# Query and key norms of the attention by one GpSimd power, and the first score product ahead of the last query transposes

## The chip, the cores and the metric

One core of a Trainium2 chip runs the whole program. The metric is the device time of one execution in microseconds (us), given as the median of the runs. A second figure, the span, is the time in the profiled execution from its first to its last recorded instruction.

## The reference, cut to what matters

The program is a two-layer diffusion transformer on 512 image tokens (the latents) and 256 context tokens, 1024 wide, all in fp32. Layer 0 mixes the tokens by attention with 16 query heads of 64 columns in 4 groups, one key and value head for each group; layer 1 mixes them by a recurrent scan. Every layer ends in a gated feed-forward block. The change lies in layer 0, between the projection of queries and keys and the first scores:

```
def rms_norm(x, w):
    xf = x.astype(jnp.float32)
    y = xf * lax.rsqrt(jnp.mean(xf * xf, axis=-1, keepdims=True) + NORM_EPS)
    return (y * w.astype(jnp.float32)).astype(x.dtype)
...
    def queries(h):
        t = h.shape[1]
        q = (h @ w_q).reshape(b, t, ATTN_KV_HEADS, ATTN_GROUP, HEAD_DIM).transpose(0, 2, 3, 1, 4)
        return rms_norm(q, q_norm)
...
    q_l = apply_axial_rope(queries(h_lat), rope)
    k_l, v_l = keys_values(h_lat)
    k_l = apply_axial_rope(k_l, rope)
    k_c, v_c = keys_values(h_ctx)
    k_all = jnp.concatenate([k_c, k_l], axis=2)
```

Each query and key head of each token is divided by the root of its mean square over 64 columns, weighted, and turned by a position angle (only the latents are turned). Then come scores, softmax, and the weighted sum of the values.

## The kernel before, in words

Tokens are handled as six tiles of 128, two to a unit: `tp` 0 and 1 are the latents, `tp` 2 is the context. A matrix product in fp32 is three products of a high and a low part (`mm3`, lines 112 to 114), so each operand is split first: ACT casts the high part (`whi_...`, L88), DVE or POOL subtracts for the low part (`wlo_...`, L91). For the query weights each group `g` has two halves of 128x1024, `wq{g}0` and `wq{g}1`; DVE makes their low parts.

The stage in question goes through 15 norm units. Twelve are query units `q{g}{tp}` (`q_first`), and between those of group 0 stand the three key units k0, k1, k2 (`k_first`). For each query unit TensorE (PE) runs 48 products `q<-...` into a PSUM bank. Then `qk_norm_rope` does, for 128 tokens x 2 tiles x 4 heads x 64 columns:

- ACT squares the bank (L510), DVE sums over 64 columns into `ss`, 128x8 (L513), and scales (L514).
- ACT takes the root (L515). DVE takes the reciprocal (L516) and makes one refining step (L517 to L520).
- DVE multiplies it in (`qhat`, L522). Then the turn: DVE multiplies by the cosine (`qrot`, L532), POOL by the sine (`qsin`, four pieces, L537), DVE adds (L541). The context has one multiplication by the weight on POOL instead (L526).
- For a query, DVE casts the high part (`qd`, L585) and POOL subtracts the low part (L586). For a key this is `kd` (L556) and `kl` (L557).

The second half of a unit is done later. PE transposes (`ptq` L592 for queries, `ptk` L567 for keys), and ACT moves the result from PSUM into `qT` or `kT` (L595, L571, L576); DVE moves one part of the keys (`kT<-ptk`, L577). The list `later` holds these second halves back by `Q_LAG` units. What is left at the end of the projections is issued in the loop of L654: query units q22, q30, q31 and q32. A score product `sc` (four products, L645 and L646) takes a query tile and all keys. PE also has filler work: `pa` (L181, the modulation vectors) and `rx` (L671, the residual's transposes).

The code states which instructions there are and what each needs. The framework's scheduler decides statically the order on each engine, so an edit can move instructions that it doesn't name. At run time each engine works strictly in its order.

Of the kernel before, what the change touches and what calls it, by code (L numbers as in the profile page):

```python
# [8 lines left out]
F32 = mybir.dt.float32  # L9
F32R = mybir.dt.float32r  # L10
U8 = mybir.dt.uint8
AF = mybir.ActivationFunctionType
ALU = mybir.AluOpType
# [3 lines left out]
P = 128  # L17
# [30 lines left out]
def kernel(  # L48
# [10 lines left out]
    PE, DVE, ACT, POOL = nc.tensor, nc.vector, nc.scalar, nc.gpsimd  # L59
    dma = nc.sync.dma_start  # L60

    def pool(name, es=None, **kw):
        return (es or ctx).enter_context(tc.tile_pool(name=name, bufs=1, reuse_waits="tile", **kw))
# [5 lines left out]
    def psum_pool(**bufs):  # L69
        es = ExitStack()  # L70
        psums["pool"], psums["bufs"] = pool(f"psum{len(bufs)}", es, space=PSUM), bufs
        return es


    def s2(name):
        if "s2" in psums:
            return psums["s2"].tile([P, 1024], F32, tag="s2", bufs=3, name=name)
        return psums["pool"].tile([P, 1024], F32, tag="s2", bufs=psums["bufs"]["s2"], name=name)
# [76 lines left out]
    mhalf = cst.tile([P, 1], F32, name="mhalf")  # L155
# [173 lines left out]
    qst = pool("qkvst", qes, side="right")  # L329
# [172 lines left out]
    def qk_norm_rope(src, tp, nm, eng=POOL):  # L502
        w, cw, sw = tabs[nm]

        def tmp(tag, bufs=1):
            tt = qst.tile([P, 512], F32, tag=tag, bufs=bufs, name=tag)
            return tt.rearrange("p (t h d) -> p t h d", t=2, d=HD)

        sq = tmp("qrot", 2)
        ACT.activation(sq, src, AF.Square)  # L510
        sst = qst.tile([P, 3, 8], F32, tag="ss", bufs=2, name="ss")
        ss, sr, sa = sst[:, 0], sst[:, 1], sst[:, 2]
        DVE.tensor_reduce(ss, sq.rearrange("p t h d -> p (t h) d"), op=ALU.add, axis=AX.X)  # L513
        DVE.tensor_scalar(ss, ss, 1.0 / HD, EPS, op0=ALU.mult, op1=ALU.add)  # L514
        ACT.activation(sr, ss, AF.Sqrt)  # L515
        DVE.reciprocal(sr, sr)  # L516
        DVE.tensor_tensor(sa, sr, sr, op=ALU.mult)  # L517
        DVE.tensor_tensor(sa, sa, ss, op=ALU.mult)
        DVE.tensor_scalar(sa, sa, -0.5, 1.5, op0=ALU.mult, op1=ALU.add)
        DVE.tensor_tensor(ss, sr, sa, op=ALU.mult)  # L520
        qh = tmp("qhat")
        DVE.tensor_tensor(qh, src, ss.rearrange("p (t h) -> p t h", t=2).unsqueeze(3).to_broadcast([P, 2, 4, HD]),  # L522
                          op=ALU.mult)
        r = tmp("qrot", 2)
        if tp == 2:
            eng.tensor_tensor(r.rearrange("p t h d -> p (t h) d"), qh.rearrange("p t h d -> p (t h) d"),  # L526
                               w.unsqueeze(1).to_broadcast([P, 8, HD]), op=ALU.mult)
            return r
        sn = tmp("qsin")
        for tt in range(2):  # L530
            t = tp * 2 + tt
            DVE.tensor_tensor(r[:, tt], qh[:, tt], cw[:, t].unsqueeze(1).to_broadcast([P, 4, HD]), op=ALU.mult)  # L532
            sn5 = sn[:, tt].rearrange("p h (a b i) -> p h a b i", a=2, b=2)
            q5 = qh[:, tt].rearrange("p h (a b i) -> p h a b i", a=2, b=2)
            t5 = sw[:, t].rearrange("p (a b i) -> p a b i", a=2, b=2)
            for b in range(2):
                POOL.tensor_tensor(  # L537
                    sn5[:, :, :, b], q5[:, :, :, 1 - b],
                    t5[:, :, b].unsqueeze(1).to_broadcast([P, 4, 2, 16]), op=ALU.mult,
                )  # L540
        DVE.tensor_tensor(r, r, sn, op=ALU.add)  # L541
        return r
# [8 lines left out]
    def k_first(tp):  # L551
        r = qk_norm_rope(kraw[tp].rearrange("p t (h d) -> p t h d", d=HD), tp, "k")
        kd = qst.tile([P, 2, KVH, 2, HD], F32R, tag="sp", bufs=3, name="kd")
        kl = qst.tile([P, 2, KVH, HD], F32R, tag="spl", name="kl")
        for i in range(2):
            DVE.tensor_copy(kd[:, :, :, i].rearrange("p t h d -> p (t h) d"), r.rearrange("p t h d -> p (t h) d"))  # L556
        POOL.tensor_tensor(kl, r, kd[:, :, :, 0].bitcast(F32), op=ALU.subtract)  # L557

        def second():
            kds = [kd[:, :, g].rearrange("p t a d -> p t (a d)") for g in range(KVH)]  # L560
            kds += [kl[:, :, 2 * i : 2 * i + 2].rearrange("p t a d -> p t (a d)") for i in range(KVH // 2)]
            cs = slice(tp * 256, tp * 256 + 256)
            for i in range(0, len(kds), 2):
                pt = bank("ptk")
                for j in range(2):
                    for tt in range(2):
                        PE.transpose(pt[:, (2 * j + tt) * P : (2 * j + tt + 1) * P],  # L567
                                     kds[i + j][:, tt].bitcast(F32), ident)
                pg = pt.rearrange("p (g t) -> p g t", g=2)
                if i < KVH:  # L570
                    ACT.copy(kTt[:, i : i + 2, cs], pg)  # L571
                    continue
                for j in range(2):
                    dst = kTt[:, KVH + j : 2 * KVH : 2, cs]
                    rows = slice(j * HD, (j + 1) * HD)
                    ACT.copy(dst[0:HD], pg[rows])  # L576
                    DVE.tensor_copy(dst[HD:P], pg[rows])  # L577

        return second

    def q_first(g, tp, ps):
        eng = DVE if g == KVH - 1 and tp == 2 else POOL
        r = qk_norm_rope(ps.rearrange("p (t h d) -> p t h d", t=2, d=HD), tp, "q", eng)
        qd = qst.tile([P, 2, 4, 2, HD], F32R, tag="sp", bufs=3, name="qd")
        DVE.tensor_copy(qd[:, :, :, g % 2], r)  # L585
        eng.tensor_tensor(qd[:, :, :, 1 - g % 2], r, qd[:, :, :, g % 2].bitcast(F32), op=ALU.subtract)  # L586

        def second():
            for tt in range(2):
                pt = bank("ptq")  # L590
                for j in range(4):
                    PE.transpose(pt[:, j * P : (j + 1) * P],  # L592
                                 qd[:, tt, j].rearrange("p a d -> p (a d)").bitcast(F32), ident)
                t = tp * 2 + tt
                ACT.copy(qT[g][:, :, t * P : (t + 1) * P], pt.rearrange("p (h t) -> p h t", h=4))  # L595

        return second
# [36 lines left out]
    def key_tiles(t):  # L634
        return range(4, 6) if t >= NLT else range(NT)

    def score_mm(h, t):
        g, j = h // 4, h % 4
        keys = key_tiles(t)
        nk, k0 = len(keys) * P, keys[0] * P  # L640
        q = qT[g][:, j, t * P : (t + 1) * P]
        ps = s2("sc")
        for a in range(0, nk, 512):
            e = min(nk, a + 512)
            PE.matmul(ps[:, a:e], q, kTh[g][:, k0 + a : k0 + e], start=True, stop=False)  # L645
            PE.matmul(ps[:, a:e], q, kTl[g][:, k0 + a : k0 + e], start=False, stop=True)  # L646
        return ps
# [1 line left out]
    dfill.drain()  # L649
    pes.close()  # L650
    pes = psum_pool(s2=2, b=2, t=2)
    early = {}
    for i, f in enumerate(later):
        f()  # L654
        if i == 0:
            early[0, i] = score_mm(0, i)
    qes.close()

    hpool = pool("hT", side="right")
# [1007 lines left out]
    sa, sb = scan_head(GH - 2), scan_head(GH - 1)  # L1667
# [72 lines left out]
```

## Time and profile before

| | before |
|---|---|
| device time, median of 3 runs | 1858.29 us (1854.88 to 1858.45) |
| the profiled execution | 1857.14 us |
| its span | 1855.4 us |
| busy PE | 1787.0 us, 96% |
| busy DVE | 1219.8 us, 66% |
| busy ACT | 766.8 us, 41% |
| busy POOL | 542.2 us, 29% |

The profiled execution has 1.74 us outside its span. A busy engine is one with an instruction under way. PE is busy nearly all the time over the whole program, but not in every stage: the norm units fill the time from about 75 to 182 us, and there it has gaps.

### The profile page before, as it was taken

What the parts mean: (1) busy time and instruction counts of PE and PEld (TensorE: products, weight loads), DVE (VectorE), ACT (ScalarE), POOL (GpSimd) and SP (SyncE); (2) the same over time, 40 slices, a digit from 0 to 9 for tenths busy, and PEclk for the clock granted to TensorE, in tenths of its full rate; (3) what the DMA queues carried; (4) which work ended last, traced back from release to release, by engine and by line L of the source; (5) the groups of instructions that cost most, each with busy time, mean ns of one, the idle gap of its engine ahead of it and who ended that gap; (6) DMA issues with size and microseconds to landing.
All of it is one profiled execution on the core that took longest, in us unless ns stands there. A gap on an engine that the chain in (4) does not pass through costs nothing.

```text
span 1855.4 us, 30297 instructions
## 1 busy us (share of the span) xinstructions
PE 1787.0 (96%) x11929; PEld 1630.3 (88%) x11929; DVE 1219.8 (66%) x2097; ACT 766.8 (41%) x1465; POOL 542.2 (29%) x508
## 2 busy tenths in 40 slices
PE   8989999998899999999999989999998999999998
PEld 6778688987899989998988989898897799898997
DVE  3576688888778777878756465655738774344443
ACT  3333777776633424242445333233333432222234
POOL 1244254444512414141314253344535100000000
PEclk9989999999999999999999999999999999999999
DMA  9433410002134242435231212213211253333321
GB/s 319 167 115 88 161 58 24 23 2 68 30 91 120 73 121 75 142 98 165 68 114 45 69 47 80 68 47 91 80 46 35 86 159 98 91 87 95 97 88 55
DMA packets 213198, 166.41 MB, mean 90 GB/s; under 512 B 7696, under 2 KB 190144, under 8 KB 213056
## 3 DMA queue, kind: packets, MB, share of 16 engines
q1 hardware_dynamic: 212768, 163.43, 28.6%
q8 instruction: 94, 1.54, 0.3%
q10 hardware_dynamic: 288, 1.05, 0.1%
q14 instruction: 48, 0.39, 0.1%
HBM read 162.36 MB, written 2.10 MB: 89 GB/s over the span
## 4 chain that ended last, share of the span: by engine, by line
PE 80%; DVE 9%; POOL 4%; ACT 4%; issue 2%; DMA 1%; POOLq 0%; SPq 0%; DVEq 0%; ACTq 0%
PE ffo L112 5%; PE ffo L113 5%; PE ffo L114 5%; PE ffi L112 4%; PE ffi L113 4%; PE ffi L114 4%; PE pt L703 3%; PE x L112 2%; PE x L113 2%; PE x L114 2%; PE lv L1541 2%; PE hz L112 2%; PE hz L113 2%; PE hz L114 2%; PE y L114 1%
## 5 line engine op out<-in xcount | busy, mean ns | idle before, releaser
L112 PE MATMUL ffi<-fnh,whi_fi 128*128 128x256 f32 x704 | 198.9, 283 | 0.1
L113 PE MATMUL ffi<-fnl,whi_fi 128*128 128x256 f32 x704 | 198.0, 281 | 1.0 <-DVE fnl L1221 1.0
L114 PE MATMUL ffi<-fnh,wlo_fi 128*128 128x256 f32 x704 | 197.8, 281 | 0.0
L113 PEld LDWEIGHTS ffi<-fnl,whi_fi 128*128 128x128 f32 x704 | 133.2, 189 | 1.5 <-DVE fnl L1221 1.4
L112 PEld LDWEIGHTS ffi<-fnh,whi_fi 128*128 128x128 f32 x704 | 132.7, 189 | 0.5 <-issue 0.3
L114 PEld LDWEIGHTS ffi<-fnh,wlo_fi 128*128 128x128 f32 x704 | 132.8, 189 | 0.0
L676 DVE SCALAR_TENSOR_TENSOR hT<-ffo,modc,hT 128x512 f32<-128x512 f32 (+1 forms) x106 | 66.9, 635 | 90.9 <-PE ffo L114 90.9
L1548 POOL TENSOR_TENSOR KD<-KD,tot 128x384 f32<-128x384 f32 x96 | 101.3, 1078 | 68.2 <-ACT kc L1531 66.6
L278 POOL TENSOR_TENSOR rc<-rc,mhalf 128x2 f32<-128x2 f32 (+2 forms) x7 | 6.2, 886 | 377.6 <-DVE rc L276 377.6
L693 POOL TENSOR_SCALAR pf<-pf,st 128x768 f32<-128x768 f32 (+1 forms) x96 | 73.3, 766 | 128.1 <-DVE st L692 91.7
L88 ACT CAST whi_fi<-raw_fi 128x1024 fp32r<-128x1024 f32 x44 | 46.2, 1051 | 146.4 <-PE ffi L113 68.7
L114 PE MATMUL ffo<-gh,wlo_w 128*128 128x512 f32 (+1 forms) x304 | 102.6, 338 | 0.0
L113 PE MATMUL ffo<-gl,whi_w 128*128 128x512 f32 (+1 forms) x304 | 102.4, 337 | 0.0
L112 PE MATMUL ffo<-gh,whi_w 128*128 128x512 f32 (+1 forms) x304 | 101.7, 337 | 0.0
L91 DVE TENSOR_TENSOR ptl<-pt,pth 128x384 fp32r<-128x384 f32 (+1 forms) x160 | 79.8, 523 | 12.4 <-ACT pth L88 11.2
L1531 ACT COPY kc<-KD 128x256 f32<-128x256 f32 x112 | 43.0, 414 | 102.8 <-PE lv L1541 37.1
L689 DVE TENSOR_REDUCE st<-sc 128x1 f32<-128x768 f32 (+1 forms) x96 | 74.1, 772 | 15.2 <-PE sc L646 12.5
L88 ACT CAST pth<-pt 128x384 fp32r<-128x384 f32 (+1 forms) x160 | 69.8, 460 | 34.4 <-PE pt L703 22.6
L235 DVE SCALAR_TENSOR_TENSOR adacc<-adw,csil,adacc 128x512 f32<-128x512 f32 x98 | 81.6, 846 | 2.6 <-DMA adw<-in_ada_w_dram 1.9
L1548 DVE TENSOR_TENSOR QD<-QD,tot 128x256 f32<-128x256 f32 x96 | 55.5, 618 | 41.2 <-PE lv L1541 40.5
L691 ACT ACTIVATE pf<-sc,st 128x768 f32<-128x768 f32 (+1 forms) x96 | 73.3, 764 | 19.3 <-DVE st L689 18.3
L703 PE MATMUL pt<-ident,pf 128*128 128x128 f32 x448 | 72.1, 275 | 5.2 <-DVE ptl L91 3.9
(833 smaller groups left out, 5985.1 us busy)
## 6 DMA issues: line engine op xcount, KB each, us to landing
raw_fi<-in_ffn_w_in_dram SPq DMA_DIRECT2D x44, 512.0 KB, 3.7
adw<-in_ada_w_dram SPq DMA_DIRECT2D x40, 512.0 KB, 4.4
adw<-in_ada_w_dram SPq DMA_DIRECT2D x80, 256.0 KB, 3.1
raw_hz<-in_hgrn_w_in_dram SPq DMA_DIRECT2D x14, 512.0 KB, 3.7
raw_fo<-in_ffn_w_out_dram SPq DMA_DIRECT2D x16, 448.0 KB, 3.8
adr<-in_ada_w_dram SPq DMA_DIRECT2D x16, 256.0 KB, 4.7
adr<-in_ada_w_dram SPq DMA_DIRECT2D x8, 512.0 KB, 6.8
raw_wq<-in_attn_w_qkv_dram SPq DMA_DIRECT2D x8, 512.0 KB, 4.9
```

The costliest lines, as they stand in the source:

```text
L88: ACT.copy(hi, src)
L91: (eng or DVE).tensor_tensor(lo, src, hi.bitcast(F32), op=ALU.subtract)
L112: PE.matmul(ps, ahi, bhi, start=first, stop=False, **kw)
L113: PE.matmul(ps, ahi, blo, start=False, stop=False, **kw)
L114: PE.matmul(ps, alo, bhi, start=False, stop=last, **kw)
L235: pin(DVE.scalar_tensor_tensor(a, raw, cc, a, op0=ALU.mult, op1=ALU.add))
L676: DVE.scalar_tensor_tensor(hT[o][:, a:e], ps, mcol(layer, ch, o, v), hT[o][:, a:e], op0=ALU.mult, op1=ALU.add)
L689: DVE.tensor_reduce(st3[:, 0:1], ps[:, :nk], op=ALU.max, axis=AX.X, negate=True)
L691: ACT.activation(pf, ps[:, :nk], AF.Exp, bias=st3[:, 0:1], accum_out=st3[:, 1:2])
L693: POOL.tensor_scalar(pf, pf, st3[:, 2:3], 1.0, op0=ALU.mult, op1=ALU.mult)
L703: PE.transpose(pt[:, i * P : (i + 1) * P], pf[:, (i0 + i) * P : (i0 + i + 1) * P], ident)
L1548: eng.tensor_tensor(view, view, f, op=ALU.mult)
```

## The change

The root, the reciprocal and the refining step (six instructions, one on ACT and five on DVE) become one POOL instruction, `ss` to the power -0.5 (`mhalf` is a constant of -0.5). The tile `ss` has 128x8 elements instead of three such rows. At the end of the projections the score product (0,0) is written ahead of the four second halves that are left over, and (0,1) stands where (0,0) stood.

```
-        sst = qst.tile([P, 3, 8], F32, tag="ss", bufs=2, name="ss")
-        ss, sr, sa = sst[:, 0], sst[:, 1], sst[:, 2]
+        ss = qst.tile([P, 8], F32, tag="ss", bufs=2, name="ss")
         DVE.tensor_reduce(ss, sq.rearrange("p t h d -> p (t h) d"), op=ALU.add, axis=AX.X)
         DVE.tensor_scalar(ss, ss, 1.0 / HD, EPS, op0=ALU.mult, op1=ALU.add)
-        ACT.activation(sr, ss, AF.Sqrt)
-        DVE.reciprocal(sr, sr)
-        DVE.tensor_tensor(sa, sr, sr, op=ALU.mult)
-        DVE.tensor_tensor(sa, sa, ss, op=ALU.mult)
-        DVE.tensor_scalar(sa, sa, -0.5, 1.5, op0=ALU.mult, op1=ALU.add)
-        DVE.tensor_tensor(ss, sr, sa, op=ALU.mult)
+        POOL.tensor_tensor(ss, ss, mhalf.to_broadcast([P, 8]), op=ALU.pow)
...
-    early = {}
+    early = {(0, 0): score_mm(0, 0)}
     for i, f in enumerate(later):
         f()
         if i == 0:
-            early[0, i] = score_mm(0, i)
+            early[0, 1] = score_mm(0, 1)
```

Lines from L516 on are six lower in the new file. Over the program DVE has 75 instructions less (15 units by five), POOL has 15 more. ACT loses the 15 roots and three loads of a function table: two ahead of the first two roots, and the one ahead of the first exponential (L691). Behind the first few score products the order is the same as before on every engine.

The first place is one unit on POOL, in the steady part: the sine product and subtraction of q31 and what follows. Before:

```order
L537 TENSOR_TENSOR qsin<-qhat,swq 128x8x16 x4
L586 TENSOR_TENSOR qd<-qrot,qd 128x8x64
L537 TENSOR_TENSOR qsin<-qhat,swq 128x8x16 x4
L586 TENSOR_TENSOR qd<-qrot,qd 128x8x64
L693 TENSOR_SCALAR pf<-pf,st_2018 128x768
```

The same place of the changed kernel:

```order
L531 TENSOR_TENSOR qsin<-qhat,swq 128x8x16 x4
L580 TENSOR_TENSOR qd<-qrot,qd 128x8x64
L514 TENSOR_TENSOR ss<-ss,mhalf 128x8
L531 TENSOR_TENSOR qsin<-qhat,swq 128x8x16 x4
L580 TENSOR_TENSOR qd<-qrot,qd 128x8x64
L514 TENSOR_TENSOR ss<-ss,mhalf 128x8
L687 TENSOR_SCALAR pf<-pf,st_1948 128x768
```

The power of each unit stands behind the subtraction of the unit ahead of it.

The second place is DVE among the first units, from the `qhat` of key unit k1 to that of query unit q01. Before:

```order
L522 TENSOR_TENSOR qhat<-kraw,ss 128x512
L532 TENSOR_TENSOR qrot<-qhat,cwk 128x256 x2
L577 CAST kT<-ptk 64x2x256
L541 TENSOR_TENSOR qrot<-qrot,qsin 128x512
L513 TENSOR_REDUCE ss<-qrot 128x8
L556 CAST kd<-qrot 128x8x64 x2
L577 CAST kT<-ptk 64x2x256
L514 TENSOR_SCALAR ss<-ss 128x8
L91 TENSOR_TENSOR wlo_wq_1140<-raw_wq_1138,whi_wq_1139 128x1024
...
L522 TENSOR_TENSOR qhat<-q_872,ss 128x512
```

The changed kernel from the same `qhat` of k1 on, to that of k2:

```order
L516 TENSOR_TENSOR qhat<-kraw,ss 128x512
L526 TENSOR_TENSOR qrot<-qhat,cwk 128x256 x2
L535 TENSOR_TENSOR qrot<-qrot,qsin 128x512
L550 CAST kd<-qrot 128x8x64 x2
L512 TENSOR_REDUCE ss<-qrot 128x8
L513 TENSOR_SCALAR ss<-ss 128x8
L516 TENSOR_TENSOR qhat<-q_862,ss 128x512
L571 CAST kT<-ptk 64x2x256
...
L512 TENSOR_REDUCE ss<-qrot 128x8
L571 CAST kT<-ptk 64x2x256
L535 TENSOR_TENSOR qrot<-qrot,qsin 128x512
```

The two moves of k0's keys out of PSUM (`kT`) stood ahead of q01's norm and now stand behind its `qhat`; the first two low parts of `wq1` stood inside q01's norm and now stand behind the `qhat` of k2, further down.

The third place is PE at the end of the query projections, from the transposes of q22 on (`ptq`, eight for each unit). Before:

```order
L592 MATMUL ptq<-ident,qd 128x128 x16
L645 MATMUL sc<-kT,qT_705 128x512
L646 MATMUL sc<-kT,qT_705 128x512
L645 MATMUL sc<-kT,qT_705 128x256
L646 MATMUL sc<-kT,qT_705 128x256
L592 MATMUL ptq<-ident,qd 128x128 x8
L671 MATMUL rx_2040<-ident,hT_2004 128x128 x2
L592 MATMUL ptq<-ident,qd 128x128 x8
L671 MATMUL rx_2040<-ident,hT_2004 128x128 x4
```

The changed kernel:

```order
L586 MATMUL ptq<-ident,qd 128x128 x8
L639 MATMUL sc<-kT,qT_705 128x512
L640 MATMUL sc<-kT,qT_705 128x512
...
L586 MATMUL ptq<-ident,qd 128x128 x8
L639 MATMUL sc<-kT,qT_705 128x512
L640 MATMUL sc<-kT,qT_705 128x512
...
L586 MATMUL ptq<-ident,qd 128x128 x16
L181 MATMUL pa<-adw_2045,cpad 32x256 x4
```

Score product (0,0) now stands ahead of q30's transposes, and (0,1) where (0,0) was. Their PSUM banks have changed with them: (0,0) had the banks of q31 and q32, and has now an idle one and that of q22; (0,1) has those of q31 and q32.

## Rows read from the trace of the kernel before

**Rows 1.** Windows: us, then busy us (x instructions) of PE, PEld, DVE, ACT, POOL; PEclk

```profile
93.00:139.00 46.00, 36.94 (x298) 33.58 (x297) 36.68 (x84) 17.35 (x33) 20.31 (x24) 0.90 0.36 116
139.00:186.00 47.00, 43.53 (x354) 42.19 (x354) 30.95 (x72) 16.20 (x33) 19.71 (x24) 0.95 0.32 89
```

**Rows 2.** Waits of PE from 60 to 240 us: total, times, longest

```profile
PE q L113 <- DVE wlo_wq L91: 5.1, 1, 5.1
PE sc L645 <- DVE qhat L522: 3.5, 1, 3.5
PE pta L189 <- ACT kT L571: 1.7, 1, 1.7
```

**Rows 3.** Chain that ended last, 70 to 240 us: start, us, what

```profile
172.78 2.15 POOL qsin L537 x4
174.95 0.70 DVE qrot L541
176.80 0.75 DVE ss L514
```

**Rows 4.** Tile ss by line: ns min/median/max, first and last start

```profile
L515 ACT ACTIVATE ss<-ss x15: 208/209/211, 77.4 to 177.6; 128x8 f32<-128x8 f32 x15
L517 DVE TENSOR_TENSOR ss<-ss x15: 166/167/1249, 77.9 to 178.1; 128x8 f32<-128x8 f32 x15
```

**Rows 5.** Timeline of DVE: start, us, what [idle before it]

```profile
93.63 0.69 DVE L522 TENSOR_TENSOR qhat<-kraw,ss 128x512 f32<-128x512 f32 x1
...
102.78 0.69 DVE L522 TENSOR_TENSOR qhat<-q,ss 128x512 f32<-128x512 f32 x1
...
134.10 1.22 DVE L91 TENSOR_TENSOR wlo_wq<-raw_wq,whi_wq 128x1024 fp32r<-128x1024 f32 x1
...
142.50 0.69 DVE L513 TENSOR_REDUCE ss<-qrot 128x8 f32<-128x512 f32 x1 [1.27 <-ACT qrot L510]
...
169.77 0.78 DVE L514 TENSOR_SCALAR ss<-ss 128x8 f32<-128x8 f32 x1
...
171.94 0.69 DVE L522 TENSOR_TENSOR qhat<-q,ss 128x512 f32<-128x512 f32 x1
...
178.93 0.69 DVE L522 TENSOR_TENSOR qhat<-q,ss 128x512 f32<-128x512 f32 x1
```

**Rows 6.** Timeline of POOL, the same columns

```profile
98.34 1.31 POOL L557 TENSOR_TENSOR kl<-qrot,kd 128x512 fp32r<-128x512 f32 x1 [1.80 <-PE ptq L592]
...
169.22 1.30 POOL L586 TENSOR_TENSOR qd<-qrot,qd 128x512 fp32r<-128x512 f32 x1 [1.33 <-DVE qd L585]
```

**Rows 7.** Powers on POOL elsewhere: the groups of L375, L278 and L1600

```profile
L375 POOL TENSOR_TENSOR rs<-rs,mhalf x6: 548/550/570, 7.2 to 14.5; 128x1 f32<-128x1 f32 x6
L278 POOL TENSOR_TENSOR rc<-rc,mhalf x7: 696/865/1189, 441.7 to 1848.9; 128x2 f32<-128x2 f32 x3, 128x3 f32<-128x3 f32 x2, 128x4 f32<-128x4 f32 x2
L1600 POOL TENSOR_TENSOR oss<-oss,mhalf x8: 1007/1314/1325, 1073.6 to 1448.9; 128x4 f32<-128x4 f32 x8
```

**Rows 8.** Timeline of PE, the same columns

```profile
99.41 0.63 PE L567 MATMUL ptk<-ident,kd 128*128 128x128 f32 x4 [0.74 <-DVE kT L577]
101.52 0.66 PE L567 MATMUL ptk<-ident,kd 128*128 128x128 f32 x4 [1.49 <-ACT qT L595]
...
135.38 0.58 PE L113 MATMUL q<-wlo_wq,hnh 128*128 128x256 f32 x1 [5.14 <-DVE wlo_wq L91]
...
179.67 0.50 PE L645 MATMUL sc<-kT,qT 128*128 128x512 f32 x1 [3.46 <-DVE qhat L522]
```

**Rows 9.** Windows of 5 us, the columns of the first group

```profile
100.00:105.00 5.00, 3.51 (x26) 1.75 (x26) 4.09 (x10) 3.88 (x7) 1.04 (x3) 0.73 0.51 133
135.00:140.00 5.00, 4.62 (x22) 4.62 (x23) 4.07 (x10) 0.21 (x1) 1.98 (x2) 0.51 0.57 162
```

**Rows 10.** Timeline of ACT, the same columns

```profile
76.09 1.28 ACT L515 ACT_TABLE_LOAD   x1
...
185.56 1.28 ACT L691 ACT_TABLE_LOAD   x1
```

## The prediction

> **What bounds the kernel now.** Over the whole program PE is busy 96%, so I looked for the stage where it is not. The windows show it: from 93 to 139 us PE is busy for 36.94 of 46 us at a granted clock of 0.90, and from 139 to 186 us for 43.53 of 47 at 0.95 [rows 1]. These are the norm units. The list of waits says what PE lacks there: 5.1 us once for the low part of a query weight (`wlo_wq`), 3.5 us once for the last `qhat`, 1.7 us for a move of keys [rows 2]; two shorter ones, 0.74 and 1.49 us, stand ahead of the transposes of k1 [rows 8]. The chain of waits runs through POOL and DVE: sine product, addition, norm [rows 3]. So DVE's norm units, one after another, set this stage: PE waits in the middle because DVE comes late to a weight (134.10 us, rows 5), and at the end because the last `qhat` is late.
>
> **The cost of one norm.** The scale of one unit ends at 169.77 + 0.78 = 170.55 and `qhat` starts at 171.94 [rows 5]: 1.39 us for root, reciprocal, refinement and two changes of engine. In their place comes a hand-over to POOL (0.15 us, from the end of `qhat` at 172.63 to the sine product at 172.78), the power, and a hand-over back (0.03 us, from 174.92 to 174.95) [rows 3, 5]. A power on 128x8 does not occur in the trace. The rows give 550 ns for one column, 696 for two, 1007 at best for four: (1007 - 550) / 3 = 152 ns for each column [rows 7]. So eight take about 1007 + 4 x 152 = 1615 ns. That makes 0.15 + 1.62 + 0.03 = 1.80 us against 1.39: **each unit's chain is 0.4 us longer**, although DVE has 0.9 us less work in it. DVE's saved time buys nothing, because in the steady units DVE has nothing between scale and `qhat` in the new order: it waits.
>
> Bounds of the power: below, eight columns cost no more than four, 1.01 us, which is 0.2 us less than now for a unit; above, powers run into others' work as those at 1325 ns did against 1007 [rows 7], so 1.62 x 1.32 = 2.13 us, 0.9 us more than now. I take 1.62, since the steps from one to four columns are even and nothing else is named in the order beside the power in a steady unit.
>
> The Trainium skill, GPSIMD Engine Reference, section 3 (and its opening), calls this engine the wrong choice for ordinary elementwise arithmetic, with Vector about twice as fast. By that, a power would take twice the 0.17 us of a DVE step, 0.34 us, a unit would gain 0.9 us, and the sum would come to about 1844 (a rival below). The trace disagrees: a single column already takes 0.55 us [rows 7].
>
> In the steady units the power isn't delayed by POOL's queue: it stands behind the subtraction of the unit before, which ended at 169.22 + 1.30 = 170.52, and DVE's scale already ended only then, at 170.55 [rows 5, 6].
>
> **The early units.** Here the change also removes a table load of 1.28 us ahead of the first root [rows 10], so k0 gains 1.28 - 0.4 = 0.9 us; q00 gives 0.4 back. In k1's norm one step lasted 1249 ns instead of 167 beside a subtraction on POOL [rows 4]; the new order puts k1's power ahead of that subtraction, so k1 gains 1.1 - 0.4. Its `qhat` moves from 93.63 [rows 5] to about 92.4. Then, with the durations of the rows: sine product 0.84 after `qhat`, 2.15 long; addition 0.7; the cast of `kd` I put at 0.7, like the addition; scale held by the subtraction `kl`, 1.31 [rows 3, 5, 6]; power and hand-overs 1.80. That is 92.4 + 0.84 + 2.15 + 0.7 + 0.7 + 1.31 + 1.8 = 99.9 for q01's `qhat`, against 102.78: 2.9 us earlier.
>
> But the moves of k0's keys, which PE's transposes of k1 need, stood ahead of q01's norm and now stand behind its `qhat`: `qhat` and one move, then cosine products of about 1.0, a sum of 0.7, the second move 0.7. They end at 99.9 + 0.7 + 0.7 + 1.0 + 0.7 + 0.7 = 103.7. PE was ready at 99.41 - 0.74 = 98.67 [rows 8]: **it waits 5.0 us in place of 0.74**. The next four transposes wait for q00's `qT` on ACT, which stands behind a squaring that needs the buffer of q01's subtraction; on POOL this now stands behind the power of k2. Addition 104.4, scale and cast to 105.0, power to 106.6, subtraction to 107.9, squaring and move 0.6 each: 109.1. PE would be there at 104.3, so it waits 4.8 us in place of 1.49. Together PE starts q10 about (5.0 - 0.74) + (4.8 - 1.49) = 7.6 us later.
>
> What it gets back: the 1.7 us wait for keys goes (k2's moves come ahead of what delayed them), and DVE reaches the weight of q20 about as now or earlier: 2.9 us ahead at q01, 0.4 back in each of four units, 134.10 - 1.3, and 1.22 long, at about 134. PE wants it at 135.38 - 5.14 + 7.6 - 1.7 = 136.1, so **the 5.1 us wait vanishes**. The clock: after the 5.14 us wait, PE had five us at a granted clock of 0.51 [rows 9], the lower of its two levels (1.2 of 2.4 GHz), which cost 2.4 us; from 100 to 105 us it had 0.73, which cost 1.35. The two new waits have only four transposes between them, so I count one slow stretch, 2.4 - 1.35 = 1.05 us. Before, PE was in effect at 135.38 + 2.4 = 137.8; after, at 136.1 + 1.05 = 137.2. **q20 starts 0.6 us earlier.** DVE waited for that unit's bank (idle 1.27 ahead of 142.50, rows 5), so the 0.6 is passed on.
>
> **The late units.** From 142.50 to the last `qhat` at 178.93 [rows 5] DVE's chain runs through six units (q20 to q32): 6 x 0.4 = **+2.4 us**.
>
> **The score product.** The four products of (0,0) took 0.8 us from 179.67, after 3.46 us of idle PE [rows 8]. Now their banks are free early and they run in that gap; it starts a little later and is as long. That is worth up to 0.8 us. (0,1) takes the old place, and brings forward work that came later. Behind it, `rx` now waits for the first exponential to free the bank; that one no longer has its table load of 1.28 us [rows 10]. I keep half, **-0.4**.
>
> **Sum.** -0.6 + 2.4 - 0.4 = +1.4 us on the profiled 1857.14, so 1858.5 us. That execution is 1.15 us under the median of 1858.29; 0.2%, or 3.7 us, is about what a measurement of this kernel can tell from no change, so the forecast is no measurable change.
>
> **Rivals.**
>
> *Slower by a dear power.* At 2.13 us a unit is 0.9 longer: 6 x 0.9 = 5.4 late; five early units delay PE by a further 5 x 0.5 = 2.5. With -0.6 - 0.4 this makes +6.9, so 1864. For it: the median of the eight powers at L1600 is 1314 ns, so most of them are not at the best [rows 7]. Against: the new order leaves DVE idle beside the power. It decides from about 1.85 us on (11 units x 0.23 = 2.5 on top of 1.4). A sentence of the Trainium skill bears on it: the GPSIMD Engine Reference, section 1, says that the engine's memory interface is shared with Vector, with contention for Vector's instructions with two inputs; the 1249 ns step agrees.
>
> *Slower by the clock.* The two early waits cost two slow stretches, 2.4 us more; or the weight of q20 is late all the same. 1861 to 1863.
>
> *Faster by a cheap power.* At 1.01 us a unit is 0.2 shorter: 6 x -0.2 = -1.2 late, 5 x -0.6 = -3 early, -0.6 and -0.8: -5.6, so 1851.5. Against: four even steps say otherwise.
>
> *Faster by ordinary arithmetic on POOL.* If a power cost as much as two of DVE's steps of 167 ns [rows 4], 0.34 us, a unit would be 0.87 us shorter, 1.28 less than in my sum; 11 units and the +1.4 make -12.7, so 1844.5. Against: 0.55 us for one column. This is the rule of the GPSIMD page of the Trainium skill named above.
>
> *Faster in the early part.* The power is as I say, but the two long waits are not: the moves of keys run earlier, and PE gains the 5.1 us wait and its slow stretch. If half of the 7.6 us goes, q20 is bound by its weight, at 134 to 135, some 3 us earlier than before: 1857.14 - 3 + 2.4 - 0.8 = 1855.7 at least, and 1853 with the slow stretch gone.
>
> *It does nothing.* The saved work was never what DVE waited for and the longer chain is met by slack: 1857.
>
> **Numbers.** The forecast and the last rival together 0.45, the dear power 0.20, the clock 0.10, the cheap power 0.09, ordinary arithmetic 0.01, the early part 0.15. Some of the last ends within 0.2%, some of the dear power too. So faster 0.24, same 0.46, slower 0.30. The range reaches from the cheap power to the dear one, 1851.5 to 1865.
>
> **What would show it.** The group of the power: median near 1.62 us. Scale to `qhat`: 1.8 us. PE's waits: two of about 5 us ahead of the transposes of k1, none for `wlo_wq`, and one of 3 to 4 us ahead of score product (0,1). The clock under 0.8 between 100 and 115 us and near 1.00 from 135 to 140. The last `qhat` 1.8 us later, near 180.7. I would be wrong first of all through the power's duration, since it counts 11 times; next, if the early waits of PE are not followed by the loss of the 5.1 us one.

## The result and the profile after

The changed kernel takes 1861.34 us (median of 10 runs, 1858.33 to 1862.84), the kernel before 1856.53 us in the same comparison (10 runs, 1854.56 to 1858.54). The ratio is 1.0026, 95% interval [1.0018, 1.0034]: 4.8 us slower, with the whole interval above 1. The forecast of 1858.5 us was "no measurable change"; the time is inside its range, 2.8 us above its point, and beyond the 0.2% in which I had placed it. The miss is larger than these 2.8 us: the forecast was a change of +1.4 us, and the change cost 4.8.

The profiled execution has a span of 1861.1 us. Windows of the changed kernel in the columns of [rows 1]:

```profile
93.00:139.00 46.00, 35.35 (x286) 32.20 (x285) 31.25 (x49) 18.06 (x30) 29.57 (x31) 0.85 0.31 101
139.00:186.00 47.00, 40.93 (x329) 40.21 (x328) 25.45 (x42) 11.51 (x21) 31.77 (x31) 0.94 0.24 73
```

PE is busy for 1.6 and 2.6 us less in the two windows of the norm units, and DVE for 5.4 and 5.5 us less. DVE's work is saved, and turned into idle time. POOL is busy for 9.3 and 12.1 us more. Waits of PE from 60 to 245 us, as in [rows 2]:

```profile
PE ptk L561 <- DVE kT L571: 6.8, 1, 6.8
PE ptk L561 <- ACT qT L589: 3.8, 1, 3.8
PE sc L639 <- DVE qhat L516: 3.3, 1, 3.3
PE q L113 <- DVE wlo_wq L91: 2.8, 1, 2.8
```

The tile `ss` by line, as in [rows 4]:

```profile
L513 DVE TENSOR_SCALAR ss<-ss x15: 160/518/775, 75.0 to 181.2; 128x8 f32<-128x8 f32 x15
L514 POOL TENSOR_TENSOR ss<-ss,mhalf x15: 1635/1636/1804, 75.3 to 182.0; 128x8 f32<-128x8 f32 x15
L516 DVE TENSOR_TENSOR qhat<-q,ss x12: 691/692/694, 86.6 to 183.7; 128x512 f32<-128x512 f32 x12
L516 DVE TENSOR_TENSOR qhat<-kraw,ss x3: 693/1742/1766, 77.0 to 107.2; 128x512 f32<-128x512 f32 x3
```

The power takes 1.64 us. The reader should also see the last line: two of the three `qhat` of the keys take over 1.7 us instead of 0.69.

The stage's start shifts by up to 1.9 us from one profile to another, so I count the stage from a marker that all kernels share, the first product after PE's short wait for `cols`, to the start of the last `qhat`. Timelines of PE and DVE; first the kernel before:

```profile
77.04 0.35 PE L112 MATMUL q<-whi_wq,hnh 128*128 128x256 f32 x1 [0.60 <-DVE cols L463]
```

and the changed kernel:

```profile
76.15 0.36 PE L112 MATMUL q<-whi_wq,hnh 128*128 128x256 f32 x1 [0.61 <-DVE cols L463]
...
181.18 0.75 DVE L513 TENSOR_SCALAR ss<-ss 128x8 f32<-128x8 f32 x1
...
183.68 0.69 DVE L516 TENSOR_TENSOR qhat<-q,ss 128x512 f32<-128x512 f32 x1 [1.75 <-POOL ss L514]
```

With the last `qhat` of [rows 5] the stage lasted 178.93 - 77.04 = 101.89 us before, and lasts 183.68 - 76.15 = 107.53 us now: **5.6 us longer, all of the loss** (the two spans differ by 1861.1 - 1855.4 = 5.7 us). From scale to `qhat` it is 183.68 - 181.93 = 1.75 us, against 1.39.

### The profile page after: what moved, and what is told of

It reads as the page before. It is cut to its first block, busy times and chain, and to the rows that moved or that the text cites. A ratio compares the mean times of both kernels' runs of the same rounds, so it can differ in the third digit from the quotient of the medians.

```text
span 1861.1 us, 30208 instructions
## 1 busy us (share of the span) xinstructions
PE 1789.2 (96%) x11929; PEld 1632.9 (88%) x11929; DVE 1208.8 (65%) x2022; ACT 761.1 (41%) x1447; POOL 568.8 (31%) x523
## 3 DMA queue, kind: packets, MB, share of 16 engines
q10 hardware_dynamic: 288, 1.05, 0.1%
## 4 chain that ended last, share of the span: by engine, by line
PE 81%; DVE 8%; POOL 5%; ACT 3%; issue 2%; DMA 0%; POOLq 0%; SPq 0%; DVEq 0%; ACTq 0%
PE ffo L112 5%; PE ffo L113 5%; PE ffo L114 5%; PE ffi L112 4%; PE ffi L113 4%; PE ffi L114 4%; PE pt L697 3%; PE x L112 2%; PE x L114 2%; PE x L113 2%; PE lv L1535 2%; PE hz L112 2%; PE hz L113 2%; PE hz L114 2%; PE sc L639 2%
## 5 line engine op out<-in xcount | busy, mean ns | idle before, releaser
L278 POOL TENSOR_TENSOR rc<-rc,mhalf 128x2 f32<-128x2 f32 (+2 forms) x7 | 6.2, 885 | 377.5 <-DVE rc L276 377.5
```

## The experiments

Three theories were set against each other. A: the order of the early units costs, since the moves of k0's keys stand behind q01's `qhat`, PE waits, and q10's norm comes late; the late units add 0.36 us each. B: only the norm's length counts, in all 15 units, 15 x 0.36 = 5.4 us. C: the moved score product costs. Each result is a ratio to the kernel before with its 95% interval; behind it stands the change of the stage, counted as above (before: 101.89 us).

**e1, sums pinned.**

```
-        DVE.tensor_reduce(ss, ...)
+        pin(DVE.tensor_reduce(ss, ...))
```

> The changed kernel with the sum over the squares (L512) of every unit pinned behind what the code issues ahead of it on DVE; this puts the moves of k0's keys back ahead of q01's norm, and all else of the change stays. Theory A (the early order: PE's transposes of k1 wait for moves that now stand behind q01's qhat, q10 comes late, and the rest is 0.36 us in each late unit): PE's waits ahead of the transposes of k1 fall from 10.6 us to under 3.5 us together, the last qhat comes 2 to 3 us earlier than in the changed kernel, and the ratio to the kernel before falls from 1.0026 to about 1.0010 to 1.0015. Theory B (only the length of the norm counts, 15 x 0.36 us, wherever the moves stand): ratio stays at 1.0026. Theory C (the moved score product is the loss): 1.0026 too.

Measured: 1.0041 [1.0029, 1.0054], stage +6.7 us. PE's waits ahead of the transposes of k1 fell from 10.6 to 2.7 + 2.3 = 5.0 us, and the kernel became no faster: the stage is longer than the 5.6 us of the change, and the intervals of the two ratios overlap. None of the theories had forecast this. Pinning also puts each sum behind the cast of the unit ahead, so this alone does not refute A; it does show that halving these waits gave nothing back here.

**e2, the power in group 0 and the keys; e3, the power in groups 1 to 3.** The old norm stands in the other units, the score products are as before.

```
-    r = qk_norm_rope(..., tp, "q", eng)
+    r = qk_norm_rope(..., tp, "q", eng, power=g == 0)   # e2; keys: True
+    r = qk_norm_rope(..., tp, "q", eng, power=g > 0)    # e3; keys: False
```

> The power in the three key units and the three query units of group 0, the old norm in the nine units after, the score product as before. The order of the early units is that of the changed kernel. Theory A: the two early waits of PE are there, 6 to 7 and 3.5 to 4.5 us, q20's weight is about 2 us late, the late units keep their length; last qhat about 2.5 us later than before, ratio about 1.0014. Theory B: six of fifteen units, 6 x 0.36 = 2.2 us less what the table load gives back, ratio 1.0005 to 1.0010, and no more wait of PE than before. Theory C: 1.000.

> The power in the nine query units of groups 1 to 3 alone, the old norm in the six units ahead of them, the score product as before. The order of the early units is that of the kernel before. Theory A: PE's early waits as before (0.7 and 1.5 us), q20's weight two units later (0.7 us), then six units of 0.36 us: last qhat 2.9 us later, ratio about 1.0015. Theory B: the same, 9 x 0.36 = 3.2 us, ratio 1.0017. Theory C: 1.000.

Measured: e2 1.0015 [1.0006, 1.0024], stage +2.4 us; e3 1.0007 [0.9998, 1.0016], stage +1.9 us. PE's waits in e2, then in e3:

```profile
PE ptk L570 <- DVE kT L580: 6.8, 1, 6.8
PE ptk L570 <- ACT qT L598: 3.8, 1, 3.8
```

```profile
PE ptq L595 <- DVE modc L191: 4.8, 1, 4.8
...
PE ptk L570 <- ACT qT L598: 1.5, 1, 1.5
...
PE ptk L570 <- DVE kT L580: 0.7, 1, 0.7
```

The two long waits come with the power in the early units, and those six units cost 2.4 us (6 x 0.36 = 2.2). Here A had the waits and the number, and B had no new wait. In e3 the six late units, from q12's `qhat` to q32's, cost 2.2 us, as both theories have it; 0.3 us had been won ahead of them by another order of DVE's work. The sum of the two, 4.3 us, is somewhat under the 5.6 of the whole change. Neither theory fits e3 as a whole: they had forecast 2.9 and 3.2 us for its stage, and PE has a new wait of 4.8 us there that neither had.

**e4, the score products alone.**

```
-    early = {}
+    early = {(0, 0): score_mm(0, 0)}
```

> The kernel before with the score products moved alone. Theories A and B: 0 to 0.8 us faster, ratio 0.9996 to 1.0000, the norm units as before to 179 us. Theory C: most of the 4.8 us, ratio 1.001 to 1.003, with new waits of PE between 180 and 200 us.

Measured: 0.9991 [0.9982, 0.9999], stage +0.1 us. This part gains a little, and C falls.

**e5, the moves of keys back.** Two orders by hand on DVE, all else as in the changed kernel:

```
+        if moves:                       # the two moves of the key unit issued last
+            behind(red, moves[0])       # the sum after the first
+            behind(hat, moves[1])       # qhat after the second
```

> The changed kernel, with two orders given by hand on DVE for each key unit: the first of its two moves of keys (L571) stands ahead of the next unit's sum, the second ahead of that unit's qhat. Pinning every sum had brought those moves forward too, but had also put each unit's sum behind the cast of the unit ahead, so it told little. Theory A (moves late, PE late, q10's norm waits for PE): the wait for the moves of k0 falls from 6.8 to under 2.5 us, q10's norm starts 2 us or more earlier than in the changed kernel, counted from the first wait of the stage, and the last qhat comes at +3 to +4 us instead of +5.6 against the kernel before; ratio 1.0014 to 1.0018. Theory B (the length of the norm alone, wherever the moves stand): 1.0026 as the changed kernel.

Measured: 1.0033 [1.0020, 1.0046], stage +5.4 us: not better than the changed kernel. PE's waits:

```profile
PE q L113 <- DVE wlo_wq L91: 8.9, 4, 3.0
PE sc L650 <- DVE qhat L522: 3.3, 1, 3.3
PE ptk L572 <- DVE kT L582: 2.2, 1, 2.2
PE ptk L572 <- ACT qT L600: 1.8, 1, 1.8
```

Its windows, in the columns of [rows 1]:

```profile
93.00:139.00 46.00, 35.68 (x288) 32.59 (x286) 29.57 (x48) 18.09 (x30) 31.57 (x31) 0.93 0.32 103
139.00:186.00 47.00, 41.18 (x336) 40.66 (x337) 25.30 (x42) 11.51 (x21) 33.34 (x32) 0.96 0.23 68
```

The wait for the moves fell from 6.8 to 2.2 us, as ordered, and four waits for weights, 8.9 us together, took its place. **Theory A falls** as the whole account: what is put earlier on DVE's chain puts something else later, and the sum stays at about 15 x 0.36 = 5.4. PE's lateness is not all undone here: its product for q10 ends 6.8 us later than before by the marker, against 10.0 in the changed kernel. But it is DVE's own chain, and no longer PE, that the sum of q10 waits for. The slow clock falls as a cause, too: the granted clock is 0.93 and 0.96, above the 0.90 and 0.95 of before, and the stage is as long as in the changed kernel.

**e8, the old norm made longer.** Two more steps of 0.2 us in each norm of the kernel before, whose early order stays:

```
         DVE.tensor_tensor(ss, sr, sa, op=ALU.mult)
+        DVE.tensor_scalar(ss, ss, 1.0, 0.0, op0=ALU.mult, op1=ALU.add)
+        DVE.tensor_scalar(ss, ss, 1.0, 0.0, op0=ALU.mult, op1=ALU.add)
```

> The kernel before with two more DVE steps on 128x8 in each norm (times one plus zero), 0.2 us each, so that each norm is 0.41 us longer while the early order, with the key moves ahead of q01's qhat, stays that of the kernel before. It asks what the length alone is worth. If the chain of DVE runs through all units, as the prediction says of the kernel before: 9 units to the weight of q20 and 6 after it, 15 x 0.41 = 6.2 us, ratio 1.0033. If only the late units count: 6 x 0.41 = 2.5 us, 1.0013.

Measured: 1.0043 [1.0030, 1.0056], stage +6.5 us, against 15 x 0.41 = 6.2. The marker, the `qhat` of q20 and the last one:

```profile
76.55 0.35 PE L112 MATMUL q<-whi_wq,hnh 128*128 128x256 f32 x1 [0.60 <-DVE cols L463]
148.72 0.69 DVE L524 TENSOR_TENSOR qhat<-q,ss 128x512 f32<-128x512 f32 x1
184.92 0.69 DVE L524 TENSOR_TENSOR qhat<-q,ss 128x512 f32<-128x512 f32 x1
```

By the marker q20's `qhat` is 72.17 - 67.74 = 4.4 us late after ten units (10 x 0.41 = 4.1), and the five units behind it add 2.0. Without a power, and with the moves of k0's keys still ahead of q01's `qhat`, the length alone costs as much as B says, early and late.

**e9, without the refining step.** The opposite test: the kernel before leaves out four DVE steps of each norm (so its root is that of ACT alone).

```
-        DVE.reciprocal(sr, sr)
+        DVE.reciprocal(ss, sr)
-        DVE.tensor_tensor(sa, sr, sr, op=ALU.mult)
-        DVE.tensor_tensor(sa, sa, ss, op=ALU.mult)
-        DVE.tensor_scalar(sa, sa, -0.5, 1.5, op0=ALU.mult, op1=ALU.add)
-        DVE.tensor_tensor(ss, sr, sa, op=ALU.mult)
```

> The kernel before without the refining step (four DVE instructions of 0.2 us in each norm; the root's own accuracy is left as it is). If the length of the norm counts in every unit, as the longer old norm suggested: 15 x 0.8 = 12 us less for DVE's chain, of which PE can take back what it waits in the stage (5.1, 3.5, 1.7, 1.5, 0.7 and some 3 us of slow clock), so 6 to 11 us faster, ratio 0.9940 to 0.9968. If the length counts only when it grows (PE or the moves of keys bound right behind): 0 to 3 us faster, ratio 0.9985 to 1.0000.

Measured: 0.9923 [0.9911, 0.9935], 14 us faster, stage -12.3 us, against -15 x 0.8 = -12. Only the total agrees: -10.1 us is won up to q20's `qhat` and 2.1 in the last five units, not 5 x 0.8, because there DVE waits for PE's products (3.9 us in four waits); and in the earlier units the scale is shorter as well, 0.17 us in the median instead of 0.55. PE's waits in it:

```profile
PE q L113 <- DVE wlo_wq L91: 1.8, 2, 1.2
...
PE sc L641 <- DVE qhat L518: 1.2, 1, 1.2
...
PE ptk L563 <- ACT qT L591: 1.0, 1, 1.0
```

PE's waits and its slow clock go with the shorter chain: both windows of [rows 1] have a granted clock of 1.00 here.

```profile
93.00:139.00 46.00, 43.23 (x378) 40.80 (x377) 36.34 (x64) 19.48 (x39) 24.48 (x29) 1.00 0.40 126
139.00:186.00 47.00, 45.37 (x381) 40.05 (x379) 27.19 (x55) 25.19 (x52) 19.35 (x24) 1.00 0.48 146
```

**e10, scale in the root, too.** It leaves out the refining step as well, and has the score products as in the changed kernel.

```
-        DVE.tensor_scalar(ss, ss, 1.0 / HD, EPS, op0=ALU.mult, op1=ALU.add)
-        ACT.activation(sr, ss, AF.Sqrt)
+        ACT.activation(sr, ss, AF.Sqrt, scale=1.0 / HD, bias=epst)
```

> As the one without refinement, and scale and epsilon given to the root on ACT instead of a DVE step of its own (L514, 0.17 us, held to 0.55 to 0.78 us by POOL), with the score products moved as in the changed kernel. It also leaves out the refining step. If DVE's chain sets the stage: another 0.4 to 0.8 us less in each unit, until PE is bound in the stage: 8 to 13 us faster than before, ratio 0.9930 to 0.9957. If PE is already bound without the refinement: the same as that one, plus at most 1 us for the score products.

Measured: 0.9946 [0.9933, 0.9958], stage -8.9 us. The ratio lies in the range of the first expectation, but the kernel is slower than e9, which neither expectation had. One wait of PE stands out:

```profile
PE ptk L562 <- ACT qT L590: 4.5, 1, 4.5
```

With this shorter chain an early wait of PE is probably no longer covered by DVE's lateness. I did not undo it by itself, so that this wait is the whole difference to e9 stays argued.

**e6, weights in the gap.** DVE waits 1.75 us for each power; here three low parts of weights are ordered into that gap, on top of e5.

```
+        at = {"wq21": 7, "wq30": 8, "wq31": 11}.get(name)   # q11, q12, q22
+        behind(halves[name], heads[at][1])                  # after the scale
+        behind(heads[at][2], halves[name])                  # before qhat
```

> As the one with the key moves ordered by hand, and the low parts of three query weights (second half of group 2, both of group 3) ordered into the gap in which DVE waits for the power: behind the scale of q11, q12 and q22 and ahead of their qhat. If the gap is free to use, each takes 1.1 us out of DVE's chain: three of them -3.4 us against the kernel with the key moves alone, ratio 0.9995 to 1.0000. If such a subtraction and the power hold each other up at the memory port, the power in those three units lasts 2.4 to 2.9 us instead of 1.64 and there is no gain.

Measured: 1.0043 [1.0028, 1.0058], stage +7.7 us. Only the last of the three lay beside a power from its start. The first had to wait for ACT's cast, and began 1.3 us after the power, which kept its 1.63 us; the second ran beside POOL's subtraction ahead of the power and drew that out to 2.20 us. The last came too late for PE, and lengthened its power. So e6 tests the gap in one unit. PE's longest wait, then DVE and POOL at that place:

```profile
PE q L117 <- DVE wlo_wq L91: 9.3, 2, 7.2
```

```profile
160.68 1.21 DVE L91 TENSOR_TENSOR wlo_wq<-raw_wq,whi_wq 128x1024 fp32r<-128x1024 f32 x1
...
160.84 2.54 POOL L524 TENSOR_TENSOR ss<-ss,mhalf 128x8 f32<-128x8 f32 x1
```

**e7, the subtraction on DVE in the gap; e11, cast and subtraction.** On top of e5, the low part of `qd` goes from POOL to DVE, behind the next unit's scale; in e11 the cast ahead of it goes there as well.

```
-        eng.tensor_tensor(qd[..., 1 - g % 2], r, qd[..., g % 2], op=ALU.subtract)
+        subs.append((cast, low))        # issued within the next unit: both on DVE
...
+            behind(one, scl)            # the cast after the scale (e7: the subtraction)
+            behind(hat, two)            # qhat after the subtraction
```

> As the one with the key moves ordered by hand, and the subtraction for the low part of qd moved from POOL to DVE, behind the scale of the next unit and ahead of its qhat, in the gap in which DVE waits for the power. POOL then doesn't hold the scale: its duration falls from 0.5 to 0.78 us to 0.17 in every query unit, and the power follows at once. If the 0.69 us of the subtraction lie beside the power, each unit from q10 on is 0.4 to 0.6 us shorter: 9 x 0.5 = 4.5 us, ratio 0.9990 to 0.9997, faster than both kernels. If the port makes power and subtraction follow each other, the unit is 0.1 to 0.3 us longer and the ratio 1.0015 to 1.0030.

> The power, with both the cast and the subtraction of the unit ahead in the gap behind the scale. The subtraction alone had lengthened the power from 1.64 to 1.94 us, since it began before the power. Now the cast of 0.43 us comes first. If only what runs on DVE as the power begins holds it up: power about 1.8 us, and 0.34 us for the cast leave the chain: a unit is 0.4 to 0.5 us shorter than with the subtraction alone, last qhat 3 to 5 us earlier, ratio 0.9985 to 0.9995. If any two-input step beside the power lengthens it by its share: power 2.0 us or more, 0.2 us shorter at most, ratio 1.0000 to 1.0010.

Measured: e7 1.0010 [1.0001, 1.0019], stage +1.2 us; e11 0.9965 [0.9953, 0.9978], stage -5.4 us. Scale and power in e7, then in e11:

```profile
L519 DVE TENSOR_SCALAR ss<-ss x15: 163/171/173, 75.5 to 177.4; 128x8 f32<-128x8 f32 x15
L520 POOL TENSOR_TENSOR ss<-ss,mhalf x15: 1633/1941/2547, 75.8 to 177.7; 128x8 f32<-128x8 f32 x15
```

```profile
L519 DVE TENSOR_SCALAR ss<-ss x15: 165/172/173, 76.9 to 172.4; 128x8 f32<-128x8 f32 x15
L520 POOL TENSOR_TENSOR ss<-ss,mhalf x15: 1636/1683/2544, 77.1 to 172.7; 128x8 f32<-128x8 f32 x15
```

The scale is no longer held in either. In e7 the subtraction begins before the power does, and the power lasts 1.94 us; in e11 the short cast is first, and it lasts 1.68. DVE in a late unit of e11:

```profile
158.72 0.69 DVE L518 TENSOR_REDUCE ss<-qrot 128x8 f32<-128x512 f32 x1 [2.07 <-ACT qrot L516]
159.44 0.17 DVE L519 TENSOR_SCALAR ss<-ss 128x8 f32<-128x8 f32 x1
159.52 0.42 DVE L596 CAST qd<-qrot 128x512 fp32r<-128x512 f32 x1
159.98 0.69 DVE L597 TENSOR_TENSOR qd<-qrot,qd 128x512 fp32r<-128x512 f32 x1
161.47 0.69 DVE L522 TENSOR_TENSOR qhat<-q,ss 128x512 f32<-128x512 f32 x1 [0.80 <-POOL ss L520]
...
167.95 0.69 DVE L522 TENSOR_TENSOR qhat<-q,ss 128x512 f32<-128x512 f32 x1 [0.80 <-POOL ss L520]
```

A unit takes 167.95 - 161.47 = 6.48 us, and here DVE waits for the square of PE's product (2.07 us). e11 computes all that the reference does and beats both kernels, by 0.35% the one before. It keeps the power and fills the gap beside it, which the change as given left empty. Part of the gain is that POOL no longer holds the scale (0.17 us in the median, against 0.52); the same two moves with the old norm were not run, so that the gain needs the power is not shown.

## Why the prediction was right or wrong

**The cost of one norm: right.** 1.64 us measured for 1.62, 1.75 from scale to `qhat` for 1.80. The even steps from one to four columns [rows 7] carried on to eight. The dear power, the cheap power and ordinary arithmetic on POOL all fell with this number. The Trainium skill, GPSIMD Engine Reference, section 3, has a measured GpSimd addition of two tensors take 1.96 times as long as Vector's; the power is dearer than that, 1.64 us against 0.17 for a DVE step on the same tile.

**The late units: right, a little small.** From q20's `qhat` to q32's the chain takes 183.68 - 146.85 = 36.83 us, against 178.93 - 144.78 = 34.15: 2.7 us more for a forecast of 2.4. Five steps of 0.36 us make 1.8 of it; 0.3 more fell at q22, and 0.5 at q30, where DVE waited 1.09 us for the square of a product that PE made late, after its 2.8 us wait for the second weight of group 3.

**The early units: the step that failed.** I let k1 gain 1.1 us because its power stands ahead of a subtraction on POOL that used to hold a step of the norm [rows 4]. The subtraction now runs beside `qhat` and holds that instead:

```profile
92.20 1.77 DVE L516 TENSOR_TENSOR qhat<-kraw,ss 128x512 f32<-128x512 f32 x1 [1.54 <-POOL ss L514]
```

Nor did k0's gain pass on: its `qhat` came 0.8 us earlier by the marker, for a forecast of 0.9, and that of q00 no earlier than before. So q01 came 1.3 us earlier (counted from the marker), not 2.9. And "2.9 us ahead at q01, 0.4 back in each of four units" treated DVE's chain to the weight of q20 as if it did not need PE. I had just made PE 7.6 us late at q10, whose norm needs that product. The kernel before, then the changed one:

```profile
110.92 1.03 PE L592 MATMUL ptq<-ident,qd 128*128 128x128 f32 x8
```

```profile
119.99 1.03 PE L586 MATMUL ptq<-ident,qd 128*128 128x128 f32 x8
...
121.72 0.68 DVE L512 TENSOR_REDUCE ss<-qrot 128x8 f32<-128x512 f32 x1
```

PE's transposes right behind q10's product start at 119.99 us, 10.0 us later than before by the marker (43.84 against 33.88); the sum of q10 follows on DVE at 121.72, behind the first low part for q20. With the marker, q10's `qhat` came 3.4 us later than before (124.35 - 76.15 = 48.20, against 121.89 - 77.04 = 44.85). The weight of q20 started at 136.12 us, 2.9 us later by the marker (59.97 against 57.06), where I had it ahead of 134.10.

**PE's waits: right in kind.** Two long waits came, 6.8 and 3.8 us (10.6 together, 9.8 forecast), the 5.1 us wait for that weight went, and 3.3 us came ahead of score product (0,1), for 3 to 4 forecast. The granted clock was as forecast, too: 0.67, 0.50 and 0.50 in the 5 us windows from 100 to 115 us, and 1.00 from 135 to 140. But q20 did not start 0.6 us earlier: PE's product for it ended 0.9 us later by the marker (65.43 against 64.57), its norm waited for DVE's own chain, and its `qhat` was 3.0 us late by the marker (70.70 against 67.74). The last `qhat`, forecast near 180.7 us, came at 183.68.

**The score product: right in sign.** e4 gains 0.09%, with an interval of 0.01 to 0.18%, which is 0.2 to 3.3 us, for a forecast of 0.4.

**The sum.** The term that failed is the -0.6 us at q20, with the gains of the early units behind it: up to q20's `qhat` I had 0.2 us won (-0.6 and its own 0.4), and 3.0 were lost. With the 2.7 of the late units that is the 5.6 us. A sum of 15 units x 0.36, 5.4 us, and nothing given back, would have come nearer. e8 shows the price of the length unit by unit. In the changed kernel the total agrees, but not the single units: by the marker, q02's `qhat` is 0.2 us early, q10's 3.4 late, q12's 2.5. That the order of the early units did it was my theory after the result, and e5 took it away as the whole account: with the moves back the stage is as long. Why the nine units of e3 cost only 1.9 us stays open.

**The number.** That the time lies inside the range says little for the mechanism. The range was wide because of the power's price, and that price was right; the miss came from the early units, from which the ends of the range were not worked out. That it still fell inside is luck. One rival has the number: "slower by the clock", 1861 to 1863. Its second condition came true, the weight of q20 was late; but PE was later still and did not wait for it. Its first, two slow stretches, is not what cost the time, by e5.

## What to carry to other kernels

Where one engine's chain of units sets a stage, a step's price is its latency from operand to operand times the units, not the work that it takes off an engine; and here time won by postponing work on that chain came back as another wait. The slower instruction on another engine paid only when the waiting engine had work ordered into the gap, and in the right order there: the first thing in the gap decided whether the two held each other up.

## What the runs showed of the hardware

A power on 128x8 on POOL lasts 1.64 us alone, 1.68 (the median) with a cast of 0.42 us on DVE at its start, 1.94 with a subtraction of 0.69 us there, and 2.54 with one of 1.21 us: it is held by what DVE began before it, and hardly by a subtraction that begins 0.2 us after it. In these rows it grows by the time that the DVE instruction still runs after the power's start, less about 0.15 us: by 0.16 us for 0.31 beside a cast in the changed kernel (1.80 us), by 0.30 for 0.44 in e7, by 0.90 for 1.05 in e6. The Trainium skill, GPSIMD Engine Reference, section 1, names the shared memory interface and contention with DVE's instructions of two inputs; the last two numbers agree. The cast has one input, and lengthened the power as well.
